# Twelve thousand constant TensorE products put ahead of a decoder layer

## The chip, the cores and the metric

The kernel runs on one core of one Trainium2 chip, as one launch. The time is the device time of that launch in microseconds (us), the median of its runs. A profile comes from one further execution of the same program, and has its own time.

The core's engines work side by side, each through its own queue in order: TensorE (PE; its weight loads are listed apart as PEld), VectorE (DVE), ScalarE (ACT), GpSimd (POOL), and SyncE (SP), which here only issues DMA transfers. Matmuls read two operands from the on-chip memory SBUF, the stationary one (the weights, loaded first) and the moving one (streamed through), and write to PSUM.

## The reference, cut to what matters

One step of a one-layer decoder over 256 prompt tokens and 8 x 4 sample tokens, 2048 wide. Conditioning vectors give six shift, scale and gate vectors by one product with `w_ada`; a gated convolution and a spatial-gating mixer follow, then a SwiGLU feed-forward part.

```python
mod = (jax.nn.silu(c) @ w_ada + b_ada).reshape(n, N_MOD, 1, D_MODEL)
h = _rms(x, g_mix) * (1 + sc_m) + sh_m
proj = h @ w_in
b_gate, c_gate, hc, u, v, ga, gb = jnp.split(proj, idx, axis=-1)
...
merged = jax.nn.sigmoid(ga) * (ya @ w_pa) + jax.nn.sigmoid(gb) * (yb @ w_pb)
x = x + gt_m * (merged @ w_out)
h2 = _rms(x, g_ffn) * (1 + sc_f) + sh_f
gate, up = jnp.split(h2 @ w_ffn_in, 2, axis=-1)
x = x + gt_f * ((jax.nn.silu(gate) * up) @ w_ffn_out)
```

All of it is float32. The outputs are the normalised `x` of both groups, the convolution state and the normalised `v` rows.

## The kernel before

All activations are kept transposed: 128 features on the partitions, 288 tokens (256 + 32) along the free dimension, so a tile of activations is 128 x 288. Weights stream from HBM through seven buffers of 128 x 2048 float32 (tag `raw`, `RAW = 7`), which are handed out in turn: whoever asks for the eighth gets the first again, and waits until all readers of the first are done.

A large product is done in three passes on float32r (`triple`, L237). ScalarE rounds a weight tile to float32r (`hi`), VectorE subtracts to get the rest (`lo`); the activation is split likewise (`split`, L309). TensorE then does high x high, high x low and low x high, each a weight load of 128 x 128 and a matmul that streams 288 columns (298 for the first tiles, which carry ten columns more). The float32r activation tiles come from `slot` (L117), which begins each of them 7 elements (`LEADIN`) into a buffer of 320 (`PITCH`). The weight tiles `hi` and `lo` are cut in pieces of 128 columns from buffers of 512.

The product with `w_ada` (class `Ada`, the matmul in L403) is different. It is plain float32 with 32 columns of conditioning vectors as weights, and four of these products lie side by side in four column groups of the array (`tile_position`). Its blocks are `a0`, `a1`, `aC` and so on; `a0[0]` is the first conditioning product of the program.

`warm` (L592) multiplies a constant bf16 tile `wb` by itself into the PSUM tile `idle`; no result of it is read. The program's steps stand in the list `steps` (L1121), in the order in which TensorE does them: `warm(24)`, `a0[0]`, `warm(5)`, `a0[1]`, the first tile of `h` (`first_tile`), the first weight stream `w0` with its opening matmuls in L525, and so on. TensorE's order is written out by hand throughout. For ScalarE, VectorE and SyncE it is written out between the opening of `head` (L1180) and its close; outside of that a planner orders them.

SyncE's queue at the start: `a0[0]`, `a0[1]`, part of `w0`, the first piece of x, the rest of `w0`, `a1[0]`, `a1[1]`, x, `wK`, `wA[0]`, x, and so on (L1182 to L1201). Each load of a weight block asks for the next `raw` buffer.

The four PSUM buffers of `psmain` (L128) are handed out in turn as well; `idle` is the first.

Of the kernel before, what the change touches and what calls it, by code (L numbers as in the profile page):

```python
# [8 lines left out]
F32 = mybir.dt.float32  # L9
F32R = mybir.dt.float32r  # L10
# [4 lines left out]
P = 128  # L15
D = 2048
T = 288
# [10 lines left out]
RAW = 7  # L28
# [60 lines left out]
def decoder_kernel(tc, d):  # L89
    nc = tc.nc  # L90
    from contextlib import ExitStack

    with ExitStack() as es:
        def pool(name, bufs=1, **kw):
            return es.enter_context(tc.tile_pool(name=name, bufs=bufs, **kw))

        pc = pool("const")
        pw = pool("wstream")
        pslot = pool("slots", MAIN)
        pkept = pool("kept", KEPT)  # L100
        ptmp = pool("tmp", 5)
        pps = pool("psum", 4, space=bass.MemoryType.PSUM)
        with tc.manual_schedule(engines={nc.tensor.engine}):
            _body(tc, nc, d, pc, pw, pslot, pkept, ptmp, pps)


def _body(tc, nc, d, pc, pw, pslot, pkept, ptmp, pps):
    ids = [0]

    def nm(s):  # L110
        ids[0] += 1
        return f"{s}_{ids[0]}"

    def const(name, shape, dt=F32):
        return pc.tile(shape, dt, tag=name, name=name)
# [12 lines left out]
    def psmain():  # L128
        return pps.tile([P, 512], F32, tag="main", name=nm("pm"), bufs=4)
# [4 lines left out]
    V, A, G, PE, SY = nc.vector, nc.scalar, nc.gpsimd, nc.tensor, nc.sync  # L134
# [232 lines left out]
    class Step:  # L367
        defer = False
        raw = None
# [218 lines left out]
    wb = const("wb", [P, 288], BF16)  # L588
    G.memset(wb, 1.0)
    idle = psmain()  # L590
# [498 lines left out]
        tail.close()  # L1089


    rh1 = h1.__getitem__
    def at(main, plan):
        out, n = [], 0
        for s in main:
            out.append(s)
            if isinstance(s, Blk):
                n += 1
                out += plan.pop(n, [])
        assert not plan  # L1100
        return out
# [71 lines left out]
    n = len(steps)  # L1173
# [30 lines left out]
    for s in steps:  # L1204
# [11 lines left out]
        i = pos[id(s)]  # L1216
# [124 lines left out]
```

## Time and profile before

| | us |
|---|---|
| median of 2 runs | 1595.74 (1595.66 to 1595.82) |
| the profiled execution | 1596.24 |
| its span, first to last instruction | 1594.5 |
| TensorE busy in it | 1583.4 |
| VectorE busy | 1015.9 |
| ScalarE busy | 735.7 |

The mean granted TensorE clock of this execution is 0.998 of full speed. The span is shorter than the time by 1.7 us, which lie around the first and the last instruction. In the lines of the profile, "L239 PE MATMUL pm<-s,hi 128\*128 128x288" is a matmul issued by line 239 that reads tiles named `s` and `hi`, writes `pm`, uses 128 rows and 128 columns of the array and streams 288 columns; "x24" counts the instructions merged in a row. The start-to-start time of two matmuls is shorter than the duration of one, because they are pipelined. A float32 matmul stands in the trace as two records, a float32r or bf16 one as one.

### The profile page before, as it was taken

What the parts mean: (1) busy time and instruction counts of PE and PEld (TensorE: products, weight loads), DVE (VectorE), ACT (ScalarE), POOL (GpSimd) and SP (SyncE); (2) the same over time, 40 slices, a digit from 0 to 9 for tenths busy, and PEclk for the clock granted to TensorE, in tenths of its full rate; (3) what the DMA queues carried; (4) which work ended last, traced back from release to release, by engine and by line L of the source; (5) the groups of instructions that cost most, each with busy time, mean ns of one, the idle gap of its engine ahead of it and who ended that gap; (6) DMA issues with size and microseconds to landing.
All of it is one profiled execution on the core that took longest, in us unless ns stands there. A gap on an engine that the chain in (4) does not pass through costs nothing.

```text
span 1594.5 us, 31602 instructions
## 1 busy us (share of the span) xinstructions
PE 1583.4 (99%) x12641; PEld 1518.7 (95%) x12641; DVE 1015.9 (64%) x2200; ACT 735.7 (46%) x1366; POOL 20.9 (1%) x65
## 2 busy tenths in 40 slices
PE   9999999999999999999999999999999999999997
PEld 8998999898998998999898999999999999999997
DVE  6676788877755667667844555555655555555565
ACT  5633344643444434456633444444444444444464
POOL 0000000000000000011000000000000000000000
PEclk9999999999999999999999999999999999999999
DMA  9887866777778766654577556443464534645341
GB/s 382 331 323 285 322 240 218 282 271 313 283 293 333 277 258 228 254 175 170 176 309 268 217 183 217 164 168 118 165 233 163 169 126 164 228 162 174 113 164 60
DMA packets 59476, 357.88 MB, mean 224 GB/s; under 512 B 6720, under 2 KB 10176, under 8 KB 28608
## 3 DMA queue, kind: packets, MB, share of 16 engines
q1 hardware_dynamic: 59040, 355.73, 60.6%
q8 instruction: 99, 1.62, 0.4%
q14 instruction: 49, 0.40, 0.1%
q10 hardware_dynamic: 288, 0.13, 0.0%
HBM read 352.74 MB, written 3.09 MB: 223 GB/s over the span
## 4 chain that ended last, share of the span: by engine, by line
PE 97%; DVE 2%; issue 0%; ACT 0%; DVEq 0%; POOL 0%; ACTq 0%; POOLq 0%
PE pm L239 30%; PE pm L244 30%; PE pm L242 30%; PE ada L403 5%; DVE lo L478 1%; PE pm L595 1%; DVE s L337 0%; DVE st L1070 0%; DVE s L318 0%; DVE t L331 0%; PE px L902 0%; ACT hi L471 0%; PE px L901 0%; PE px L213 0%; PE px L848 0%
## 5 line engine op out<-in xcount | busy, mean ns | idle before, releaser
L239 PE MATMUL pm<-s,hi 128*128 128x288 f32 (+1 forms) x3750 | 1095.4, 292 | 0.3 <-DVE s L998 0.3
L242 PE MATMUL pm<-s,hi 128*128 128x288 f32 (+1 forms) x3750 | 1090.6, 291 | 0.1
L244 PE MATMUL pm<-s,lo 128*128 128x288 f32 (+1 forms) x3738 | 1088.1, 291 | 0.0
L471 ACT CAST hi<-raw 128x512 fp32r<-128x512 f32 (+1 forms) x963 | 585.5, 610 | 774.2 <-PE pm L242 738.2
L478 DVE TENSOR_TENSOR lo<-raw,hi 128x512 fp32r<-128x512 f32 (+1 forms) x849 | 578.6, 683 | 420.0 <-ACT hi L471 407.6
L239 PEld LDWEIGHTS pm<-s,hi 128*128 128x128 f32 x3750 | 702.1, 187 | 15.7 <-issue 13.3
L242 PEld LDWEIGHTS pm<-s,hi 128*128 128x128 f32 x3750 | 702.2, 187 | 0.3 <-DVE s L337 0.3
L244 PEld LDWEIGHTS pm<-s,lo 128*128 128x128 f32 x3738 | 699.9, 187 | 0.0
L258 DVE TENSOR_TENSOR lo<-raw,hi 128x512 fp32r<-128x512 f32 x111 | 74.6, 676 | 28.0 <-ACT hi L471 27.2
L403 PE MATMUL ada<-raw,cs 128*32 128x512 f32 (+2 forms) x1152 | 88.0, 452 | 0.0
L403 PEld LDWEIGHTS ada<-raw,cs 128*32 128x32 f32 x1152 | 30.9, 110 | 44.5 <-issue 41.6
L793 DVE TENSOR_TENSOR s<-pm,s 128x288 f32<-128x288 f32 x72 | 32.8, 456 | 18.5 <-PE pm L244 18.2
L311 ACT CAST s<-t 128x288 fp32r<-128x288 f32 (+1 forms) x76 | 32.9, 433 | 19.1 <-DVE t L825 12.5
L313 DVE TENSOR_TENSOR s<-t,s 128x288 fp32r<-128x288 f32 (+1 forms) x76 | 35.0, 461 | 6.5 <-ACT s L311 5.7
L353 DVE SCALAR_TENSOR_TENSOR x<-pm,mod,x 128x256 f32<-128x256 f32 x79 | 37.5, 475 | 0.0
L991 DVE SCALAR_TENSOR_TENSOR t<-t,pm 128x288 f32<-128x288 f32 x42 | 19.1, 454 | 19.3 <-PE pm L244 19.3
L785 DVE TENSOR_TENSOR s<-pm,s 128x288 f32<-128x288 f32 x48 | 21.8, 454 | 9.9 <-PE pm L244 9.2
L352 DVE TENSOR_TENSOR t<-pm,mod 128x32 f32<-128x32 f32 x79 | 15.1, 192 | 16.5 <-PE pm L244 15.9
L776 DVE TENSOR_TENSOR s<-s,rb 128x288 f32<-128x288 f32 x48 | 21.5, 448 | 0.0
L181 ACT ACTIVATE t<-x 128x288 f32<-128x288 f32 x29 | 12.9, 444 | 17.4 <-DVE x L356 17.4
L186 DVE TENSOR_TENSOR acc<-acc,t 128x288 f32<-128x288 f32 x33 | 15.0, 455 | 8.2 <-ACT t L181 8.2
L770 DVE SCALAR_TENSOR_TENSOR s<-pm,s 128x256 f32<-128x256 f32 x36 | 17.3, 481 | 2.7 <-PE pm L244 2.7
(168 smaller groups left out, 479.5 us busy)
## 6 DMA issues: line engine op xcount, KB each, us to landing
raw<-in_fi SPq DMA_DIRECT2D x84, 1024.0 KB, 4.8
raw<-in_a SPq DMA_DIRECT2D x64, 1024.0 KB, 7.5
raw<-in_f SPq DMA_DIRECT2D x64, 704.0 KB, 4.0
raw<-in_wD SPq DMA_DIRECT2D x34, 1024.0 KB, 5.3
raw<-in_aE SPq DMA_DIRECT2D x16, 1024.0 KB, 9.8
raw<-in_wo SPq DMA_DIRECT2D x16, 1024.0 KB, 5.8
raw<-in_wC SPq DMA_DIRECT2D x19, 768.0 KB, 4.4
raw<-in_pa SPq DMA_DIRECT2D x8, 1024.0 KB, 6.0
```

Source lines behind the costliest of these rows:

```text
L239: PE.matmul(out, wh, ah, start=first, stop=False)
L242: end_ = PE.matmul(out, wh, al, start=False, stop=turn and last)
L244: end_ = PE.matmul(out, wl, ah, start=False, stop=last)
L258: lows.pop(0)[1]()
L311: A.copy(hi, a)
L313: V.tensor_tensor(lo, a, hi.bitcast(F32), ALU.subtract)
L353: V.scalar_tensor_tensor(x[:, m, :TP], ps[:, :TP], mod[:, gt0 + m, 0:1], x[:, m, :TP], ALU.mult, ALU.add)
L403: PE.matmul(acc[32 * j : 32 * j + 32, :w], cs[:, kt, :], self.raw[:, o : o + w], start=kt == 0, stop=kt == 15, tile_position=(0, 32 * j), ...
L471: A.copy(hi, self.raw[:, s * 128 : e * 128])
L478: sub()
L785: return V.tensor_tensor(part[m], ps[:, :T], part[m], ALU.add)
L793: V.tensor_tensor(a, ps[:, :T], a, ALU.add)
```

## The change

Ahead of `steps`, a new function `bench` is defined and called. It takes four `raw` buffers, sets one (`f`) to 0.75, and copies it into three float32r tiles: `r0` on VectorE, `r1` and `r2` on ScalarE. It takes the three `psmain` buffers beside `idle`. Then TensorE multiplies pieces of these tiles into PSUM, and nobody reads the results. In the order of the code:

| group | matmuls | streamed columns |
|---|---|---|
| `wb` by itself, bf16 | 48 | 288 |
| pairs of products on 64 rows each, in two row groups (`rowed`); 16 starts x 10 x 2 | 320 | 288 |
| widths 290 and 292, 64 starts of the moving operand x 14 each | 1792 | 290, 292 |
| two-level access patterns of 2 and of 36 pieces, 16 starts x 14 each | 448 | 288 |
| 8 starts of the moving operand x 16 drawn weight starts x 6 x 3 | 2304 | 288 |
| 400 drawn places of weights and moving operand x 6 x 3 | 7200 | 288 |
| sum | 12112 | |

The program after it is the same.

```diff
+    def bench():
+        import random
+
+        f = pw.tile([P, 2048], F32, tag="raw", name=nm("bench"), bufs=RAW)
+        V.memset(f, 0.75)
+        rs = []
+        for i in range(3):
+            r = pw.tile([P, 2048], F32R, tag="raw", name=nm("benchr"), bufs=RAW)
+            A.copy(r, f) if i else V.tensor_copy(r, f)
+            rs.append(r)
+        r0, r1, r2 = rs
+        outs = [idle] + [psmain() for _ in range(3)]
+
+        def mm(s, m, n=T):
+            PE.matmul(idle[:, :n], s, m, start=True, stop=True)
+
+        def w(r, k, s=0):
+            return r[:, P * (k % 12) + s : P * (k % 12) + s + P]
+
+        def mv(r, o, n=T):
+            return r[:, o : o + n]
+
+        def rowed(step, o, count):
+            for i in range(count):
+                for j in range(P // step):
+                    rows = slice(step * j, step * j + step)
+                    PE.matmul(
+                        outs[j][:, :T],
+                        w(r0, i)[rows],
+                        mv(r2, o)[rows],
+                        start=True,
+                        stop=True,
+                        tile_position=(step * j, 0),
+                        skip_group_check=True,
+                    )
+
+        for i in range(48):
+            mm(wb[:, :P], wb)
+        for o in range(3, 64, 4):
+            rowed(64, o, 10)
+        for n in (290, 292):
+            for o in range(64):
+                for i in range(14):
+                    mm(w(r0, i), mv(r2, o, n), n)
+        for q in (2, 36):
+            for o in range(3, 64, 4):
+                for i in range(14):
+                    PE.matmul(
+                        idle[:, :T].rearrange("p (a b) -> p a b", a=q),
+                        w(r0, i),
+                        mv(r2, o).rearrange("p (a b) -> p a b", a=q),
+                        start=True,
+                        stop=True,
+                    )
+        rng = random.Random(3)
+        for a in range(7, 64, 8):
+            for b in rng.sample(range(64), 16):
+                for i in range(6):
+                    mm(w(r0, i), mv(r2, a))
+                    mm(w(r1, i, b), mv(r2, a))
+                    mm(w(r0, i), mv(r2, 512 + a))
+        for i in range(400):
+            s, l = rng.randrange(8), rng.randrange(64)
+            a, b = (8 * rng.randrange(8) + (7 - s) for _ in range(2))
+            for i in range(6):
+                mm(w(r0, i, s), mv(r2, s + a))
+                mm(w(r0, i, s), mv(r2, 512 + s + b))
+                mm(w(r1, i, s + l), mv(r2, s + a))
+
+    bench()
     rh1 = h1.__getitem__
```

## The prediction

> **What bounds the kernel now.** I read the page first, for the busy shares, the granted clock and the chain.
>
> ```profile
> PE 1583.4 (99%) x12641; PEld 1518.7 (95%) x12641; DVE 1015.9 (64%) x2200; ACT 735.7 (46%) x1366; POOL 20.9 (1%) x65
> ...
> PEclk9999999999999999999999999999999999999999
> ...
> PE 97%; DVE 2%; issue 0%; ACT 0%; DVEq 0%; POOL 0%; ACTq 0%; POOLq 0%
> ```
>
> TensorE is busy in 99% of the span, it holds 97% of the chain that ended last, and its clock is granted in full in every slice. So there is no gap of any size in which more TensorE work could hide: 1594.5 us of span less 1583.4 us busy leaves 11 us, most of it at the two ends. A matmul added to this queue is paid for by its start-to-start time. The mean duration in the groups (292 ns for L239) is not that time, since one matmul overlaps the next. The windows give the pace, and the timeline gives it for the wider form:
>
> ```profile
> core 0: us, PE busy (x), PEclk, DMA share, GB/s
> ...
> 900.00:1500.00 600.00, 600.00 (x4631) 1.00 0.50 170
> ...
> 25.09 0.29 PE L239 MATMUL pm<-s,hi 128*128 128x298 f32 x1
> ...
> 28.70 0.29 PE L239 MATMUL pm<-s,hi 128*128 128x298 f32 x1
> ```
>
> From 900 to 1500 us there is almost nothing but 288 columns in fp32r with a new weight tile each: 600 us / 4631 = 129.6 ns. Between the two quoted starts of 298 columns lie 27 matmuls: 3.61 us / 27 = 133.7 ns. Ten columns cost 4.1 ns, 0.41 ns a column, so at this width the pace follows the columns streamed and not the weight load.
>
> **The start of the program**, the only place that the change touches otherwise (timeline):
>
> ```profile
> 0.83 0.17 DVE L158 MEMSET ones<- 128x128 f32 x1 [0.83 <-PEq L1320]
> 1.08 0.48 DVE L162 MEMSET cs<- 128x512 f32 x1
> 1.13 5.94 PE L595 MATMUL pm<-wb 128*128 128x288 bf16 x24 [1.13 <-POOL wb L589]
> 4.74 0.32 ACT L164 ACTIVATE t<-t 128x144 f32<-128x144 f32 x1 [1.80 <-DMA t<-in_c]
> 5.44 0.24 DVE L166 TENSOR_SCALAR cs<-t 128x144 f32<-128x144 f32 x1
> 7.00 1.12 PE L403 MATMUL ada<-raw,cs 128*32 128x64 f32 x64
> 10.78 1.15 PE L595 MATMUL pm<-wb 128*128 128x288 bf16 x8
> 12.09 0.80 PE L525 MATMUL pm<-s,hi 128*128 128x298 f32 x4 [0.16 <-ACT s L701]
> 18.34 1.10 PE L403 MATMUL ada<-raw,cs 128*32 128x64 f32 x64
> 19.17 0.51 ACT L471 CAST hi<-raw 128x384 fp32r<-128x384 f32 x1 [2.58 <-DMA raw<-in_wK]
> ```
>
> The reader is to see two paces of the same bf16 warm-up matmul. Of the first 24, all but the last take (5.94 - 0.45) / 23 = 239 ns each; of the eight at 10.78, (1.15 - 0.29) / 7 = 123 ns. The last matmul's own length, 448 and 282 ns, is taken off by this row:
>
> ```profile
> L595 PE MATMUL pm<-wb x54: 282/292/448, 1.1 to 1585.4; 128*128 128x288 bf16 x54
> ```
>
> The clock row shows nothing of this, but the first 6 us of matmuls run at half pace, whatever they are.
>
> **The change part by part.** It removes nothing, and adds 12112 matmuls to TensorE ahead of the first warm-up step, one DVE memset and three copies (one DVE, two ACT) of 2048 elements, and takes four of the seven `raw` buffers first.
>
> *Getting the constants.* DVE's memset of `f` stands behind L166, which ends at 5.68. From the two memset rows, 128 elements in 0.17 us and 512 in 0.48, 2048 take about 1.76 us: `f` is there at 7.4. The casts:
>
> ```profile
> L471 ACT CAST hi<-raw 128x512 fp32r<-128x512 f32 x892 | 549.8, 618 | 712.8 <-PE pm L242 680.3 <-PE pm L244 9.8 <-DMA raw<-in_fi 5.2
> L471 ACT CAST hi<-raw 128x384 fp32r<-128x384 f32 x66 | 33.8, 512 | 59.8 <-PE pm L242 57.3 <-DMA raw<-in_wK 2.6
> ```
>
> 128 elements more cost 106 ns, so 2048 cost 618 + 12 x 106 = 1890 ns. ACT makes `r1` and then `r2`: 7.4 + 1.9 + 1.9 = 11.2. DVE makes `r0` beside it. The 48 new bf16 matmuls run from 1.13: 25 at 239 ns until 7.1, 23 at 123 ns until 9.9. So they are hidden but for nothing, and the first fp32r product begins at about **11.3 us** (9.9 if the memset is put ahead of L165, where DVE waits 3.5 us anyway).
>
> *Row-tiled, 320.* 160 pairs of 64 rows. No row of the trace is row-tiled. The nearest are the conditioning products, tiled by columns, four side by side:
>
> ```profile
> 287.63 4.50 PE L403 MATMUL ada<-raw,cs 128*32 128x512 f32 x40
> 292.06 0.40 PE L239 MATMUL pm<-s,hi 128*128 128x288 f32 x1
> ```
>
> 40 records of 512 columns take 4.43 us, 111 ns each, which is 4.6 columns in a ns, against 2.2 for L239: tiles do run beside one another. Bounds: one after another at 129.6 is 41.5 us, a pair in the time of one is 20.7 us. I take **20.7**, the row of tiles being the nearest. The Trainium skill, "TensorEngine Tiling (Array Packing)", section Key Properties, says that different tiles can load weights and multiply in parallel, and that changing the tiling mode drains the engine. By the first half the sum is the one taken; the trace agrees for tiles by column (4.6 columns in a ns), and shows none by row.
>
> *290 and 292 columns, 1792.* 896 x (129.6 + 2 x 0.41) + 896 x (129.6 + 4 x 0.41) = 116.9 + 117.6 = **234.5 us**.
>
> *Two-level patterns, 448* (2 x 144 and 36 x 8, both contiguous): the same columns, **58.1 us** at 129.6.
>
> *288 columns at drawn places, 2304 + 7200 = 9504*: **1231.7 us** at 129.6.
>
> What the trace doesn't show is another starting place: all fp32r moving tiles of this kernel start 7 elements into a slot of 320 (`slot`, L117). From below, the price of a 288-column matmul is bounded by the bf16 one at 123 ns, which streams as many columns; from above by the 298-column one at 133.7, as though a bad place cost ten columns. 129.6 lies between them, and it is the row of the very same type and width, so I take it. On some 11744 matmuls outside the row tiles, the ends are -78 and +48 us.
>
> *After it.* The sum of the fp32r part is 20.7 + 234.5 + 58.1 + 1231.7 = 1545.0, so it ends at B = 11.3 + 1545.0 = 1556.3. `warm(24)` now runs at full pace, 24 x 123 = 2.95 us, and the first L403 stands at B + 2.95 = 1559.3, where it stood at 7.00 before. **The shift is 1552.3 us**; of it 10.2 us is the later start and -2.9 us the warm-up that no longer runs at half pace.
>
> *Queues.* `f`, `r0`, `r1`, `r2` sit in four of seven buffers, so the second half of `a1` needs the buffer of `r0`, which is read to the end. SP's queue stops there until B, and behind it stand x, wK and the wA loads. Cost nothing, and this is the cover: `a0`, `w0`, the first x and half of `a1` landed long before B. `a1[1]` is read at 18.34 in the row above, 11.34 after the first L403, so at B + 14.3; wK is read at 19.17, so B + 15.1.
>
> ```profile
> raw<-in_a SPq DMA_DIRECT2D x8, 512.0 KB, 6.9
> ...
> raw<-in_wK SPq DMA_DIRECT2D x1, 384.0 KB, 8.9
> ...
> GB/s 382 331 323 285 322 240 218 282 271 313 283 293 333 277 258 228 254 175 170 176 309 268 217 183 217 164 168 118 165 233 163 169 126 164 228 162 174 113 164 60
> ```
>
> `a1[1]` (1 MB), x (0.14) and wK (0.38) are 1.6 MB, 4 us at 382 GB/s, and with a landing of up to 8.9 us they are there by B + 13. If that cover went, all later work would move by the lateness, a few us. The 2.6 us wait for wK at 19.17 should go; ACT is then early and TensorE waits 0.3 us less at most, which I leave out. PSUM: the three more `psmain` buffers are written by TensorE before and after, in its own order, so nobody waits.
>
> *Sum.* The profiled execution took 1596.24 us (span 1594.5), 0.5 above the median 1595.74. 1595.7 + 1552.3 = **3148 us**.
>
> **The rivals.**
>
> *Places cost more.* A start off the shown one breaks the stream of one operand, and the drawn matmuls run nearer to 133.7 ns. Nothing in the trace speaks against it, since only one place is there. At 133.7 for the 11744: 3148 + 48 = 3196 us. It decides from about 3 ns a matmul (35 us).
>
> *Places cost less.* With no VectorE or ScalarE work beside it and constant data, fp32r goes at the bf16 pace of 123 ns: 3148 - 78 = 3070 us. Against it: 129.6 holds at 900 to 1500 us, where DVE is half idle. The Trainium skill, "TensorE: Matmul & The Clock Gate", section Back-to-back issue gap, gives N / 2.4 + 2.5 ns for a warm matmul, 122.5 ns here, by which the sum would be some 3065 us. The trace agrees for bf16 (123 ns) and not for fp32r (129.6).
>
> *A form leaves the one-pass pace.* Row tiles, two-level patterns or odd weight starts could be cut up as plain fp32 is:
>
> ```profile
> 428.33 0.60 PE L848 MATMUL px<-cp,s 128*128 128x128 f32 x4
> 428.65 0.19 PEld L239 LDWEIGHTS pm<-s,hi 128*128 128x128 f32 x1
> 428.68 0.38 PE L239 MATMUL pm<-s,hi 128*128 128x288 f32 x1
> ```
>
> Two fp32 products of 128 columns (four records) take 0.35 us, 1.37 ns a column, three times L239's 0.45. For the 768 row-tiled and two-level matmuls at 394 ns each: 3148 - 79 + 303 = 3372 us.
>
> *The matmuls are dropped*, as no result is read, and the time is not slower: 1595.7 us, with at most the casts' start added, some 1600. It decides once fewer than 32 us / 0.1296 = 246 of the 12112 are left. Against it stands the row of L595: 54 warm-up matmuls, whose results nobody reads either, are all in the trace.
>
> **How the numbers follow.** My forecast, within 3 ns a matmul of the shown pace (3113 to 3183 us): 0.66. Places cost more: 0.18. Places cost less: 0.09. A form at fp32's pace: 0.06. Dropped: 0.01. For 8 in 10 the range takes the forecast and most of the first rival, its 48 us with the 21 us of row tiles in turn: 3148 + 69 = 3217; below, it ends at 3105, which leaves the third rival out. A measurement of this kernel tells 2% from no change; all cases but the last are far beyond it. Slower by over 2%: 0.98; within 2%: 0.01; faster: 0.01, as no row gives a way to it.
>
> **What would show it.** In the profile after: some 12100 more matmuls, the new lines first in time; a window in the drawn part with about 772 matmuls in 100 us right, 750 for the first rival, 810 for the second; the row-tiled group over 21 us in all or over 41; the fp32r part beginning at 10 to 11.5 us; the first L403 to the first L525 still 5.1 us apart; the stages after it as long as before; the granted clock at 1.0. What would make it wrong above all is a price of the weights' place, which the last 7200 vary and no row here shows.

## The result and the profile after

The changed kernel takes 3167.2 us (3166.8 to 3167.6, two runs) against 1595.74: a ratio of 1.985, with a 95% interval of 1.976 to 1.993. Forecast were 3148 us, 3105 to 3217. The profile of the changed kernel has a span of 3165.8 us. Its page first: busy shares, the slices of clock and DMA, and the chain by engine and by line.

```profile
PE 3155.0 (100%) x24753; PEld 3088.9 (98%) x24753; DVE 1019.5 (32%) x2202; ACT 739.4 (23%) x1368; POOL 21.1 (1%) x65
...
PEclk9999999999999999999999999999999999999999
DMA  1000000000000000000088767776557554544543
...
PE 98%; DVE 2%; ACT 0%; issue 0%; DVEq 0%; POOL 0%; ACTq 0%; POOLq 0%
PE pm L1106 47%; PE pm L239 15%; PE pm L242 15%; PE pm L244 15%; PE ada L403 3%; PE pm L1139 2%; PE pm L1118 1%; DVE lo L478 0%; PE pm L595 0%; DVE s L337 0%; DVE st L1070 0%; DVE s L318 0%; ACT hi L471 0%; DVE acc L186 0%; DVE s L793 0%
```

There are 12112 more matmul records, as many as were added, so nothing was dropped. TensorE is busy to the end at full granted clock, and DMA stands still for half the span: SyncE's queue waits for its buffer. The new groups, kept apart by form (here the busy time of a group is nearly its share of the span, since it has TensorE to itself), and the pace in the drawn part:

```profile
L1106 PE MATMUL pm<-benchr,benchr 128*128 128x288 f32 x9504 | 1245.1, 293 | 0.0
...
L1106 PE MATMUL pm<-benchr,benchr 128*128 128x292 f32 x896 | 121.2, 297 | 0.0
L1106 PE MATMUL pm<-benchr,benchr 128*128 128x290 f32 x896 | 120.3, 296 | 0.0
...
L1139 PE MATMUL pm<-benchr,benchr 128*128 128x288 f32 x448 | 58.8, 293 | 0.0
...
L1118 PE MATMUL pm<-benchr,benchr 64*128 64x288 f32 x320 | 21.2, 290 | 0.0
...
900.00:1500.00 600.00, 600.00 (x4581) 1.00 0.00 1
```

4581 matmuls in 600 us are 131.0 ns each, where the kernel's own products take 129.6. The start, from the timeline:

```profile
1.13 8.67 PE L1106 MATMUL pm<-wb 128*128 128x288 bf16 x48 [1.13 <-POOL wb L589]
...
1.94 1.76 DVE L1096 MEMSET bench<- 128x2048 f32 x1 [0.37 <-issue]
...
5.12 3.68 ACT L1100 CAST benchr<-bench 128x2048 fp32r<-128x2048 f32 x2
...
9.73 6.55 PE L1118 MATMUL pm<-benchr,benchr 64*128 64x288 f32 x96
```

The planner put the memset ahead of the wait for L164, so both casts are done by 8.8, within the 48 bf16 products, and the fp32r part begins at 9.73. And the end of the added part:

```profile
1575.66 3.11 PE L595 MATMUL pm<-wb 128*128 128x288 bf16 x24
1575.72 1.14 SPq L385 DMA_DIRECT2D raw<-in_a  x2
...
1577.43 0.38 SPq L454 DMA_DIRECT2D raw<-in_wK  x1
...
1578.70 1.10 PE L403 MATMUL ada<-raw,cs 128*32 128x64 f32 x64
...
1583.77 0.80 PE L525 MATMUL pm<-s,hi 128*128 128x298 f32 x4 [0.15 <-ACT s L701]
...
1588.11 0.56 ACT L471 CAST hi<-raw 128x384 fp32r<-128x384 f32 x1
```

SyncE issues `a1[1]`'s load at 1575.72, the moment that `r0` is free. From the first L403 to the first L525 lie 5.07 us, as before (5.09). Matched in TensorE's order, the matmuls after it stand 1571.7 us later than before at the first L403, 1571.6 at the 1000th and 1571.4 at the last.

| part, by the starts in the trace | forecast us | measured us | off by |
|---|---|---|---|
| fp32r part begins at | 11.3 | 9.7 | -1.6 |
| row-tiled, 320 | 20.7 | 21.1 | +0.4 |
| 290 and 292 columns, 1792 | 234.5 | 241.2 | +6.7 |
| two-level, 448 | 58.1 | 58.7 | +0.6 |
| drawn places, 9504 | 1231.7 | 1245.0 | +13.3 |
| everything after, against before | -2.9 | -3.1 | -0.2 |

The last row is the shift of the last matmul (1571.4) less that of the first warm-up step (1574.5, from 1.13 to 1575.66). The sum is +19.2 us, the whole distance of 3148 and 3167.2. Nearly all of it is the pace of the matmuls at places that the kernel itself does not use.

### The profile page after: what moved, and what is told of

Its sections match the earlier page's. It is cut to its first block, busy times and chain, and to the rows that moved or that the text cites. A ratio compares the mean times of both kernels' runs of the same rounds, so it can differ in the third digit from the quotient of the medians.

```text
span 3165.8 us, 55834 instructions
## 1 busy us (share of the span) xinstructions
PE 3155.0 (100%) x24753; PEld 3088.9 (98%) x24753; DVE 1019.5 (32%) x2202; ACT 739.4 (23%) x1368; POOL 21.1 (1%) x65
## 4 chain that ended last, share of the span: by engine, by line
PE 98%; DVE 2%; ACT 0%; issue 0%; DVEq 0%; POOL 0%; ACTq 0%; POOLq 0%
PE pm L1106 47%; PE pm L239 15%; PE pm L242 15%; PE pm L244 15%; PE ada L403 3%; PE pm L1139 2%; PE pm L1118 1%; DVE lo L478 0%; PE pm L595 0%; DVE s L337 0%; DVE st L1070 0%; DVE s L318 0%; ACT hi L471 0%; DVE acc L186 0%; DVE s L793 0%
## 5 line engine op out<-in xcount | busy, mean ns | idle before, releaser
L1106 PE MATMUL pm<-benchr,benchr 128*128 128x288 f32 (+2 forms) x11296 | 1486.4, 293 | 0.0
L1106 PEld LDWEIGHTS pm<-benchr,benchr 128*128 128x128 f32 x11296 | 1486.1, 188 | 0.2 <-issue 0.2
L239 PE MATMUL pm<-s,hi 128*128 128x288 f32 (+1 forms) x3750 | 1096.0, 292 | 0.3 <-DVE s L998 0.3
L242 PE MATMUL pm<-s,hi 128*128 128x288 f32 (+1 forms) x3750 | 1091.4, 291 | 0.1
L244 PE MATMUL pm<-s,lo 128*128 128x288 f32 (+1 forms) x3738 | 1088.8, 291 | 0.0
L239 PEld LDWEIGHTS pm<-s,hi 128*128 128x128 f32 x3750 | 702.5, 187 | 15.7 <-issue 13.3
L242 PEld LDWEIGHTS pm<-s,hi 128*128 128x128 f32 x3750 | 702.6, 187 | 0.3 <-DVE s L337 0.3
L244 PEld LDWEIGHTS pm<-s,lo 128*128 128x128 f32 x3738 | 700.2, 187 | 0.0
L403 PE MATMUL ada<-raw,cs 128*32 128x512 f32 (+2 forms) x1152 | 88.0, 452 | 0.0
L403 PEld LDWEIGHTS ada<-raw,cs 128*32 128x32 f32 x1152 | 30.8, 110 | 44.3 <-issue 41.6
L1139 PE MATMUL pm<-benchr,benchr 128*128 128x288 f32 x448 | 58.8, 293 | 0.0
L1139 PEld LDWEIGHTS pm<-benchr,benchr 128*128 128x128 f32 x448 | 58.7, 188 | 0.0
L793 DVE TENSOR_TENSOR s<-pm,s 128x288 f32<-128x288 f32 x72 | 32.9, 457 | 18.5 <-PE pm L244 18.2
```

The costliest lines, as they stand in the source:

```text
L239: PE.matmul(out, wh, ah, start=first, stop=False)
L242: end_ = PE.matmul(out, wh, al, start=False, stop=turn and last)
L244: end_ = PE.matmul(out, wl, ah, start=False, stop=last)
L403: PE.matmul(acc[32 * j : 32 * j + 32, :w], cs[:, kt, :], self.raw[:, o : o + w], start=kt == 0, stop=kt == 15, tile_position=(0, 32 * j), ...
L1106: PE.matmul(idle[:, :n], s, m, start=True, stop=True)
L1139: PE.matmul(idle[:, :T].rearrange("p (a b) -> p a b", a=q), w(r0, i), mv(r2, o).rearrange("p (a b) -> p a b", a=q), start=True, stop=True,)
```

## The experiments

**Is it the place?** The drawn part once at the kernel's own places, once at a start of the moving tile that was slow in the two-level group. A place is counted here from the last multiple of 64 elements in SBUF. By the addresses in the built program all fp32r activation tiles of the kernel begin at 23 (16, and the 7 of `LEADIN`), the high weights at 0 and the low ones at 40. The constant tiles of the added part begin at 0, so the number behind `r2` is the moving start itself.

```diff
-        rng = random.Random(3)
-        for a in range(7, 64, 8):
...
+        for i in range(3168):
+            mm(w(r0, i), mv(r2, 23))
+            mm(w(r0, i), mv(r2, 512 + 23))
+            mm(w(r1, i, 40), mv(r2, 23))
```

> The outputs are computed in full. The 9504 drawn matmuls are replaced by as many at the places that the kernel's own products have: moving tile 23 elements past a multiple of 64, weights at 0, 0 and 40. After took 3167.2 us, and its drawn part 1245.0 us by the trace (131.0 ns each). Theory (the place of the operands sets the pace): the drawn part runs at the kernel's own 129.6 ns, 1231.7 us, and the time is 3154 us. Rival (something else in the added part slows it: constants, the same bank of PSUM each time, no accumulation): 131.0 ns as before, 3167 us.

The second kernel has 35 in place of 23, and no 40.

> The outputs are computed in full. The 9504 drawn matmuls are replaced by as many with the moving tile 35 elements past a multiple of 64 and all weights at 0, where the trace of after has 133.3 ns in its two-level group. Theory (the place sets the pace): 9504 x 133.3 = 1267 us in place of 1245, and the time is 3189 us. Rival (place is noise, the two-level group's starts differ for another reason): 131.0 ns, 3167 us.

Measured, in one run each: 3154.0 and 3190.6 us. The group of the drawn matmuls, first at 23, then at 35:

```profile
L1106 PE MATMUL pm<-benchr,benchr 128*128 128x288 f32 x9504 | 1232.2, 291 | 0.0
```

```profile
L1106 PE MATMUL pm<-benchr,benchr 128*128 128x288 f32 x9504 | 1267.3, 295 | 0.0
```

9504 x 129.6 = 1231.7 and 9504 x 133.3 = 1266.9, while the fp32r groups ahead of it take 321.0 us in both and in the changed kernel. At the kernel's places a constant, unread product costs what a real one does. The rival falls: neither the constants nor the one PSUM bank nor the missing accumulation slows the added part.

**Do the row groups run side by side?**

```diff
-                    rows = slice(step * j, step * j + step)
+                    rows = slice(0, step)
...
-                        tile_position=(step * j, 0),
+                        tile_position=(0, 0),
```

> The outputs are computed in full. The 320 matmuls of 64 rows all use the first row group and the first 64 rows, where after lets each pair use two groups. Theory (the two groups of a pair run side by side): now each takes a full step of some 130 ns, 41.5 us in place of 21.1, and the time is 3187.5 us. Rival (a matmul on half the rows is cheaper by itself): 21 us as before, 3167 us.

Measured: 3188.3 us, 21.1 more. The row-tiled group, which had 21.2 us:

```profile
L1118 PE MATMUL pm<-benchr,benchr 64*128 64x288 f32 x320 | 42.1, 289 | 0.0
```

A matmul on half the rows is no cheaper; two of them in two row groups take the time of one. What the Trainium skill, "TensorEngine Tiling (Array Packing)", section Key Properties, says of tiles that work in parallel, this run shows for rows: 66.1 ns each against 131.5.

**What does the stop of SyncE's queue cost without its cover?** The added part holds all seven buffers to its end.

```diff
+        held = [pw.tile([P, 256], F32, tag="raw", name=nm("held"), bufs=RAW, padded_shape=[P, 2048]) for _ in range(3)]
+        for h in held:
+            G.memset(h, 0.75)
...
+        for h in [f] + held:
+            PE.matmul(idle[:, :P], h[:, :P], h[:, P : 2 * P], start=True, stop=True)
```

> The outputs are computed in full. The added part holds all seven raw buffers to its end (three more small tiles, and four more float32 products of 128 columns that read them, about 1 us), so that no weight of the layer can be loaded before the end. Theory (the loads that landed in the shadow of the added part are what hides the stop of SyncE's queue): the first conditioning product waits for its load, some 6 us after the end of the added part in place of 3, and the waits of the start of before come back: 3167.2 + 1 + 3 to 5 = 3171 to 3174 us. Rival (the loads are early enough anyway): 3168 us.

Measured: 3169.6 us, 2.4 more. The end of its added part (timeline):

```profile
1575.25 1.82 SPq L385 DMA_DIRECT2D raw<-in_a  x4
...
1576.08 3.10 PE L595 MATMUL pm<-wb 128*128 128x288 bf16 x24
...
1579.11 0.65 PE L403 MATMUL ada<-raw,cs 128*32 128x64 f32 x32
1580.26 0.65 PE L403 MATMUL ada<-raw,cs 128*32 128x64 f32 x32 [0.50 <-DMA raw<-in_a]
```

The two profiles differ by 2.0 us (spans of 3167.8 and 3165.8). The four products take 0.9 us, but the added part's fp32r products had begun 0.5 us earlier (at 9.26), so the warm-up starts 0.4 later, at 1576.08 in place of 1575.66. The rest are waits: the first half of L403 comes 3.0 us after the start of the warm-up, as in the changed kernel, and only the second half waits. Matched in order, the later work is 0.7 us further back there, 1.0 at `a1` and 1.6 from the 350th record on. So the cover is worth some 1.6 us, which is neither the theory's price nor the rival's nothing. My 3 to 5 took the 6 us that lie before L403 in the kernel before for the time of the load; it lands in under 4 (issued 1575.25, read 1579.11).

**Which part of the place?** The drawn part cut into 16 sections of 594, one form each, such as:

```diff
+        for i in range(594):
+            PE.matmul(idle[:, :T], w(r0, i), mv(r2, 23), start=True, stop=True)
+        for i in range(594):
+            PE.matmul(idle[:, :T], w(r0, i, 40), mv(r2, 23), start=True, stop=True)
+        for i in range(594):
+            PE.matmul(idle[:, :T], w(r0, i), mv(r2, 35), start=True, stop=True)
```

> The outputs are computed in full. The 9504 drawn matmuls are replaced by 16 sections of 594, one form each, so that each shows its own pace. Theory (place of moving and stationary operand together): 288 columns at moving 23 with weights at 0: 130.0 ns, at moving 35 with weights at 0: 133.3 ns, at moving 39 with weights at 0: 130 to 131 ns; moving 35 with weights at 12 (the distance of 23 and 0) goes back to 130 if the distance counts, stays at 133.3 if the moving place alone does; the same weight piece each time, accumulation, or another PSUM bank each time leave 133.3. Rival (PSUM or the start flag sets the pace): those last two differ from 133.3 by over 1 ns and the places do not. Widths 280, 296, 304 and 320 at 23: by 0.41 ns a column from 130.0, 126.7, 133.3, 136.6 and 143.1 ns; if a width that is no multiple of 8 is what made 290 and 292 dear, these four lie on that line.

Some of the 16 groups. L1147 and L1149: start 23 with weights at 0 and at 40. L1151 to L1161: start 35 with weights at 0, at 40, the same piece each time, at 12, accumulated, in four banks in turn; two of them are shown. L1163 to L1167: starts 24, 0 and 16. L1171 and L1177: 280 and 320 columns at 23.

```profile
L1177 PE MATMUL pm<-benchr,benchr 128*128 128x320 f32 x594 | 87.3, 308 | 0.0
...
L1155 PE MATMUL pm<-benchr,benchr 128*128 128x288 f32 x594 | 79.4, 295 | 0.0
...
L1161 PE MATMUL pm<-benchr,benchr 128*128 128x288 f32 x594 | 79.4, 295 | 0.0
...
L1163 PE MATMUL pm<-benchr,benchr 128*128 128x288 f32 x594 | 78.4, 294 | 0.0
...
L1147 PE MATMUL pm<-benchr,benchr 128*128 128x288 f32 x594 | 77.4, 291 | 0.0
L1149 PE MATMUL pm<-benchr,benchr 128*128 128x288 f32 x594 | 77.4, 291 | 0.0
L1171 PE MATMUL pm<-benchr,benchr 128*128 128x280 f32 x594 | 75.4, 288 | 0.0
```

Start to start these are 130.0 ns at 23, 133.3 at 35 in all six sections, 131.7 at 0, 16 and 24. In a steady stream of one form the start of the moving tile decides. Weights at 0, 40 and 12, a weight load of the same piece, accumulation and the bank change nothing, and the distance of the two operands doesn't either (35 with 12 stays at 133.3). Widths 280, 288, 296 and 304 lie on a line, 126.7, 130.0, 133.3 and 136.7: 0.417 ns a column. 320 does not: 146.7 where the line has 143.3.

In a mixed order the weights are not without effect. The first 2304 drawn products of the changed kernel keep one moving start over 288 matmuls, while one product in three has its weights at one of 16 drawn places, 18 matmuls for each. Start to start these groups of 18 took 130.0 to 135.6 ns at start 63, 131.1 to 133.3 at 15 and 129.6 to 131.1 at 23. The dearest, with weights at 48, repeats 131, 138, 138 ns: the product at 48 and the one after it are slow, while the groups just before and after it run at 131.1 and 130.0. Whether 48 itself does this, or the change of place from one product to the next, no run separates.

**All 64 starts, and the order in which they come.**

```diff
+        up, down, wide = 66, 66, 264
+        for i in range(up):
+            mm_ = PE.matmul(idle[:, :T], w(r0, i), mv(r2, 0), start=True, stop=True)
+        for i in range(up):
+            mm_ = PE.matmul(idle[:, :T], w(r0, i), mv(r2, 1), start=True, stop=True)
...
```

> The outputs are computed in full. The 9504 drawn matmuls are replaced by 288-column ones with weights at 0 and the moving tile at each of 64 starts, 66 at each, once going up and once going down, and then 264 each of 290, 292, 294 and 298 columns at start 23. Theory (the start alone sets the pace): the way up and the way down give the same for each start, to 0.3 ns; 23 and 39 130.0, 0, 16 and 24 131.7, 35 133.3; some of the 64 may be below 130.0, and the mean of those 7 past a multiple of 8 is that of the drawn part, 131.0. Rival (the stream has several lasting rhythms, and which one it falls into depends on what came before): some starts differ by over 1 ns between the two ways. Widths at 23: if only the place counts, 130.8, 131.6, 132.5 and 134.1 by 0.41 ns a column; if the width counts up to the next 8, 133.3 for 290, 292 and 294.

Start to start, worked out from the trace, with the mean of the eight starts of each remainder:

```
start modulo 8       7      3      4      0      2      6      1      5
way up, ns       131.4  131.4  132.2  132.7  133.4  134.3  135.0  135.7
way down, ns     130.7  131.5  131.8  132.7  133.3  134.1  134.7  135.4
```

No start is under 130.0, and the mean of all is 133.1. Some groups (66 each): start 23 up (L1194) and down (L1356), 35 up (L1218) and down (L1332), 19 up (L1186) and down (L1364), 37 up (L1222) and down (L1328).

```profile
L1222 PE MATMUL pm<-benchr,benchr 128*128 128x288 f32 x66 | 9.4, 303 | 0.0
L1328 PE MATMUL pm<-benchr,benchr 128*128 128x288 f32 x66 | 9.0, 298 | 0.0
L1332 PE MATMUL pm<-benchr,benchr 128*128 128x288 f32 x66 | 9.0, 295 | 0.0
L1364 PE MATMUL pm<-benchr,benchr 128*128 128x288 f32 x66 | 9.0, 295 | 0.0
L1218 PE MATMUL pm<-benchr,benchr 128*128 128x288 f32 x66 | 8.9, 295 | 0.0
...
L1186 PE MATMUL pm<-benchr,benchr 128*128 128x288 f32 x66 | 8.7, 291 | 0.0
L1194 PE MATMUL pm<-benchr,benchr 128*128 128x288 f32 x66 | 8.7, 292 | 0.0
...
L1356 PE MATMUL pm<-benchr,benchr 128*128 128x288 f32 x66 | 8.7, 291 | 0.0
```

Both theories hold in part. Most starts have one pace both ways, 23, 35, 39 and 0 among them. Eleven of the 64 differ by over 1 ns: 19 runs at 130.0 going up and at 133.2 going down, 37 at 139.7 and 134.7. So a stream at one start can hold either of two rhythms over 66 matmuls, by what came before. The widths 290, 292, 294 and 298 at start 23 took 131.1, 133.3, 131.1 and 138.6 ns, which is neither the line nor steps of eight.

**Does it hold for the real products?** The kernel before, without the added part, with its activation tiles begun elsewhere; four kernels, each with one number changed.

```diff
-LEADIN = 7
+LEADIN = 19
```

> The kernel before without the added part, its outputs computed in full; the float32r activation tiles begin 19 elements into their buffers in place of 7, which moves them from 23 to 35 past a multiple of 64. Theory (the place of the operands sets the pace of any float32r product, with real data too): 10878 products of 288 columns at up to 133.3 ns in place of 129.6; the high weights lie at 0, where 35 was slow, the low ones at 40, which no run has shown, so 10 to 41 us more: 1606 to 1637 us. Rival (the place matters only in a bare stream of constants): 1596 us.

> The kernel before without the added part, its outputs computed in full; the float32r activation tiles begin at the start of their buffers, 16 past a multiple of 64. Theory (the place sets the pace): a time of its own, between that of 23 and that of 35; the 290-column group of after has 133.1 ns at 16 and 131.5 at 23, which would be 1596 + 11328 x 1.6 ns = 1614 us. Rival (place matters only in a bare stream of constants): 1596 us.

> The kernel before without the added part, its outputs computed in full; the float32r activation tiles begin 5 elements into their buffers, 21 past a multiple of 64. Theory (the map of 64 starts holds for the kernel's own products): 136.6 ns both ways at 21, 7.0 ns over the kernel's 129.6, on 10878 products of 288 columns: 1596 + 76 = 1672 us. Rival (in the kernel's order of three products only some starts, 35 and 16 among them, are slow, by a few ns and not by the map): 1596 to 1640 us.

> The kernel before without the added part, its outputs computed in full; the float32r activation tiles begin 20 elements into their buffers, 36 past a multiple of 64. Theory (the map holds): 131.1 on the way up and 130.0 ns on the way down at 36, 0.4 to 1.5 ns over the kernel's pace: 1600 to 1613 us. Rival (the kernel's order has a pace of its own at each start): any time from 1590 to 1670 us outside of that.

The windows from 900 to 1500 us in these kernels, in the order of the table below (before: x4631). The third is from 930 to 1530, as up to 930 there are 48 records of L403 in it:

```profile
900.00:1500.00 600.00, 600.00 (x4502) 1.00 0.50 171
```

```profile
900.00:1500.00 600.00, 600.00 (x4527) 1.00 0.49 168
```

```profile
930.00:1530.00 600.00, 600.00 (x4357) 1.00 0.47 163
```

```profile
900.00:1500.00 600.00, 600.00 (x4540) 1.00 0.49 169
```

| tiles start at | us | ratio to before, 95% interval | ns a matmul | the map, up / down |
|---|---|---|---|---|
| 35 (`LEADIN` 19) | 1635.8 | 1.0248 (1.0231 to 1.0265) | 133.3 | 133.1 / 133.2 |
| 16 (`LEADIN` 0) | 1625.8 | 1.0189 (1.0174 to 1.0204) | 132.5 | 132.2 / 131.7 |
| 21 (`LEADIN` 5) | 1683.6 | 1.0547 (1.0531 to 1.0563) | 137.7 | 136.5 / 136.6 |
| 36 (`LEADIN` 20) | 1623.7 | 1.0173 (1.0156 to 1.0190) | 132.2 | 131.1 / 130.0 |

So the place matters for real data too, by up to 5.5% of the kernel; all four intervals lie above 1. From 930 to 1500 us no step from one matmul to the next is over 141 ns in any of them, so it is the products that are slower, and not a wait here and there. Only 35 came as expected (1606 to 1637 us). 16 took 1625.8 us where 1614 was expected, 21 took 1683.6 where 1672 was, and 36 took 1623.7, out of its 1600 to 1613, as its rival had it. The map of the bare stream gets 35 right and ranks 16 and 21 rightly, but is 0.3 to 0.8 ns short at 16, 1.1 at 21 and 1.1 to 2.2 at 36. The kernel's order, two moving tiles and two weight tiles in turn, has a rhythm of its own at a start: at 36 a step takes 134.2 ns from L239, 132.5 from L242 and 130.0 from L244, though the moving tile begins at 36 in all three. The same is seen at 23, where it gives 129.6 and the bare stream 130.0. No start that was tried is faster than the kernel's, so no version came out that beats the kernel before.

## Why the prediction was right, and where it was off

**What bounds it.** Right: with TensorE busy in 99% of the span, 12112 matmuls are paid for in full, and the stages after them were the same to 0.3 us.

**The pace.** This is the term that was mis-sized: "129.6 lies between them, and it is the row of the very same type and width, so I take it". At the kernel's own places that price is exact (1232.2 us with 23, 0 and 40). At drawn places it is 131.0, 13.3 us more in all, and that is the rival *places cost more*, at a third of its 4.1 ns. So the step that failed is the one that took the pace of one place for all places. That it cost so little is luck and not my working: the drawn starts are all 7 past a multiple of 8, which the code says and I didn't use. The map has 130.7 to 131.4 for those, against 133.1 over all and 135.5 for those 5 past, at which the same 9504 products would have cost about 56 us over my 129.6. The map does not give the drawn part start by start either: at 15 its first 288 products took 131.8 ns where the map has 133.3. The weights' place, which I had named as the main danger, moved single groups by up to 5.6 ns (63 with weights at 48); what it adds to the sum no run separates.

**290 and 292 columns.** The slope of 0.41 ns a column was right as a mean: over 64 starts, 288 columns take 133.3 on the way up, and 290 and 292 took 134.1 and 135.1. What was 6.7 us short is again the base, since this group goes through all 64 starts and I priced it at one. As a price of columns at one start the slope does not hold: at 23 the bare stream takes 8.6 ns more for 298 columns than for 288, and the kernel's own order 3.7 (in the trace the 27 steps that I read as 3.61 us are 3.600, 133.3 ns each).

**The lower bound** of 123 ns was reached by no fp32r group of 288 columns on 128 rows: the lowest of any was 129.6. It belongs to *places cost less*, the second rival, which the prediction calls the third where it gives the range. The Trainium skill's gap of N / 2.4 + 2.5 ns ("TensorE: Matmul & The Clock Gate", section Back-to-back issue gap) has the slope that 280 to 304 columns show (0.417), and for fp32r a base 7.5 ns too low (126.7 against 119.2 at 280).

**Row tiles** were taken at the pair in the time of one: 20.7 against 21.1, and the run with one row group shows the price of the other bound, 42.1.

**The two-level patterns** cost what flat ones do at the same starts (58.7 us, 131.0 ns each, where the map has 131.3). No form left the one-pass pace.

**The start** was 1.6 us early, by the case that I had put in brackets: the memset went ahead of L165. **The warm-up** at full pace and **SyncE's queue** came as forecast; the cover that I named is real, but worth 1.6 us.

## What to carry to other kernels

A price read from one place of a kernel holds for that place. Before it is used for operands that begin elsewhere in SBUF, the place is worth a run of its own: here the start of the moving fp32r tile alone moved a TensorE-bound kernel by 1.7 to 5.5%. That run should have the products in their real order, since a bare stream at the same start was up to 2.2 ns a product off. Two products on half the rows should go to two row groups, where they take the time of one; in one group they take twice that.

## What was not expected of the hardware

The start of the moving tile within 64 elements sets the pace of fp32r products of 288 columns, from 130.0 to 139.7 ns in a bare stream, while weights at 0, 12 or 40 leave a steady stream as it is. The paces are not spread evenly: many starts have 130.0, 133.3 or 136.7, which are 3.33 ns apart, the price of eight columns, with a few in between (131.1, 131.7, 135.6). At some starts the stream keeps either of two paces. No run shows what makes these paces, nor what the weights' place does in a mixed order, nor why the kernel's order of three products is 0.4 ns faster at 23 and up to 2.2 ns slower at 36 than the bare stream.

The first matmuls of a program run at half pace for a time that differs: the same 48 bf16 products took 8.7 us in the changed kernel, and 7.4 and 8.1 us in the runs at 23 and 35. In the three traces the record of the granted clock begins only at 6.5, 4.0 and 5.3 us, within 0.1 us of the first step at 123 ns, so the clock rows of the page can't show the half pace.
